# A softmax over 512 columns: the three-row tile moves from the head of the work to its end

## The chip, the cores and the metric

The kernel runs on one core of one Trainium2 chip. The metric is the device time of one execution in microseconds (us); lower is better. Durations in this document come from a hardware profile of one execution; PE is TensorE, DVE VectorE, ACT ScalarE, POOL GpSimd and SP SyncE.

## The reference

The input is one array of 16 x 1024 rows with 512 float32 values each. Every row is halved and put through a softmax:

```python
def reference(x: np.ndarray) -> np.ndarray:
    temp = 2.0
    x_scaled = x / temp
    x_max = np.max(x_scaled, axis=-1, keepdims=True)
    exp_x = np.exp(x_scaled - x_max)
    return (exp_x / np.sum(exp_x, axis=-1, keepdims=True)).astype(np.float32)
```

The input is 33.55 MB and the output as much. Each byte is read once and written once.

## The kernel before

The 16,384 rows are 128 rows on each of the 128 partitions, and "row" below means one such row of 512 values on all partitions, 256 KB. The rows are cut into ten tiles, listed in `TILES` (L10) with their number of rows and their place in `arena`, an on-chip buffer of 98 rows: tiles of 3 and 5 rows, and then eight of 15. Each tile is one contiguous piece of memory. The last two tiles, 8 and 9, go to places that earlier tiles have used; `LATE` (L14) says which stores must have landed before: those of tiles 0, 1 and 2 for tile 8, that of tile 3 for tile 9.

The work of a tile goes over four engines.

- **Loads** (`load`, L113). SP issues the load of tile 0 and ACT that of tile 1 ahead of the opening barrier (`early`, L153). Behind the barrier ACT issues the loads of tiles 2 to 7 (`loads`, L157), one after the other, with no wait. POOL issues those of tiles 8 and 9 (L176 to L179): it first waits until the exponentials of 83 rows are done (`TURN`), and then for the stores in `LATE`. The tile numbered `SPREAD`, tile 1, is loaded in three transfers: all rows but the last over 128 partitions, then the last row over 126 partitions, and over the remaining 2.
- **Exponentials** on ACT, in place, one instruction for each row; it also writes the row's sum to `stats`. The kernel takes exp(x/2) without subtracting the maximum first. Three rows of the first tile are written out (L201 to L208), and the rest runs in a loop over chunks of `E` = 5 rows (`exponentials`, L259). Before each chunk ACT waits for a count that PE raises when a tile has landed (L193, L194).
- **Reciprocal and multiply** on DVE (L166, L169), over up to three chunks of one tile at once, so 15 rows in one multiply; in the last tile each chunk of 5 is multiplied by itself.
- **Stores** on SP, tile by tile in order (`store`, L135), each waiting for its tile's last multiply.

Each engine's order is thus fixed by the program text, and the engines meet at semaphores only. Transfers run on three queues: SP's (q1 in the profile), ACT's (q10) and POOL's (q0). Within a queue they start in the order in which they were issued.

At the end the kernel tests that all sums were in a sound range (L180 to L190). A flag is read by DVE, ACT and POOL when the last store but one has landed (`rounds`, L142 to L148); if a sum had been out of range, a second path with the maximum subtracted would follow. With this input it doesn't run. SP ends by waiting for all stores (L256, L257).

Of the kernel before, what the change touches and what calls it, by code (L numbers as in the profile page):

```python
# [7 lines left out]


TILES = [  # L10
    (3, 0), (5, 3), (15, 8), (15, 23), (15, 38), (15, 53), (15, 68), (15, 83), (15, 0), (15, 15),
]

LATE = {8: (0, 1, 2), 9: (3,)}  # L14
ARENA = 98

HEAD = [3]
E = 5

SPREAD = 1  # L20

TURN = 83

LO, HI = 1.0, 1.0e30
G = 64
# [3 lines left out]
def kernel(  # L29
# [5 lines left out]
    nc = tc.nc  # L35
# [3 lines left out]
    Exp = mybir.ActivationFunctionType.Exp  # L39
# [6 lines left out]
    n_rows = N // P  # L46
    assert sum(r for r, _ in TILES) == n_rows

    arena = nc.alloc_sbuf_tensor("arena", (P, ARENA, D), fp32)
    stats = nc.alloc_sbuf_tensor("stats", (P, n_rows), fp32)  # L50
# [10 lines left out]
    for r, at in TILES:  # L61
        assert at == base % ARENA
        tiles.append((base, r, at))
        base += r

    def dram(ap, t):
        b, r, _ = tiles[t]
        return ap[b * P : (b + r) * P].rearrange("(p r) d -> p r d", r=r)

    def sb(t):  # L70
        _, r, at = tiles[t]
        return arena[:, at : at + r, :]

    straight = sum(HEAD)
    sizes = HEAD + [E] * ((n_rows - straight) // E)
    starts = [sum(sizes[:k]) for k in range(len(sizes))]
    assert sum(sizes) == n_rows
    owner = [max(t for t, (b, _, _) in enumerate(tiles) if b <= s) for s in starts]
# [12 lines left out]
    ld = [nc.alloc_semaphore(f"ld{t}") for t in range(len(tiles))]  # L91
    s_home = {t: nc.alloc_semaphore(f"s_home{t}") for t in LATE}
    s_near = nc.alloc_semaphore("s_near")
    s_end = nc.alloc_semaphore("s_end")
    s_exp = nc.alloc_semaphore("s_exp")
    s_go = nc.alloc_semaphore("s_go")
# [16 lines left out]
    def load(eng, t):  # L113
        r = tiles[t][1]
        parts = [(0, P, 0, r)]
        if t == SPREAD:
            parts = [(0, P, 0, r - 1), (0, 126, r - 1, r), (126, P, r - 1, r)]
        for p, q, lo, hi in parts:
            eng.dma_start(  # L119
                out=sb(t)[p:q, lo:hi], in_=dram(xf, t)[p:q, lo:hi]  # L120
            ).then_inc(ld[t], 16)

    stored_by = {u: s_home[t] for t, us in LATE.items() for u in us}
    for t, (_, r, at) in enumerate(tiles):
        over = {u for u, (_, ru, au) in enumerate(tiles[:t]) if at < au + ru and au < at + r}
        assert over <= {u for v, us in LATE.items() if v <= t for u in us}

# [11 lines left out]
    def take(eng, sem, n):  # L139
        eng.wait_ge(sem, n).then_inc(sem, -n)  # L140
# [11 lines left out]

    def early():  # L153
        load(nc.sync, 0)
        load(nc.scalar, 1)

    def loads():  # L157
        for t in range(2, min(LATE)):
            load(nc.scalar, t)

    def program():

        for j, ks in enumerate(pairs):
            b, c = starts[ks[0]], sum(sizes[k] for k in ks)
            a = b % ARENA
            nc.vector.reciprocal(  # L166
                out=recip[:, b : b + c], in_=stats[:, b : b + c]
            )._wait_ge(s_exp, ks[-1] + 1).then_inc(s_rec, 1)
            nc.vector.tensor_mul(  # L169
                out=arena[:, a : a + c],  # L170
                in0=arena[:, a : a + c],
                in1=recip[:, b : b + c].unsqueeze(2).to_broadcast([P, c, D]),
            )._wait_ge(s_rec, j + 1).then_inc(s_mul, 1)

        nc.gpsimd.memset(ones[:, :], 1.0).then_inc(s_ones, 1)  # L175
        nc.gpsimd.wait_ge(s_exp, starts.index(TURN))  # L176
        for t, us in LATE.items():
            nc.gpsimd.wait_ge(s_home[t], landings(us))
            load(nc.gpsimd, t)  # L179
        nc.gpsimd.tensor_scalar(  # L180
            out=inside[:, :], in0=stats[:, :], scalar1=LO, scalar2=HI,
            op0=Alu.max, op1=Alu.min,
        )._wait_ge(s_exp, len(sizes)).then_inc(s_cnt, 1)
        nc.vector.scalar_tensor_tensor(  # L184
            out=inside[:, :], in0=inside[:, :], scalar=1.0, in1=stats[:, :],
            op0=Alu.mult, op1=Alu.is_equal, accum_out=count[:, :],
        )._wait_ge(s_cnt, 1).then_inc(s_cnt, 1)
        nc.vector.tensor_scalar(  # L188
            out=flag[:, :], in0=total[:, :], scalar1=float(N), scalar2=None, op0=Alu.is_ge,
        )._wait_ge(s_tot, 1).then_inc(s_flag, 1)  # L190


        for t in range(len(tiles)):  # L193
            nc.tensor.wait_ge(ld[t], 48 if t == SPREAD else 16).then_inc(s_go, owner.count(t))  # L194
        nc.tensor.wait_ge(s_ones, 1)
        nc.tensor.matmul(  # L196
            total[:, :], lhsT=count[:, :], rhs=ones[:, :], start=True, stop=True
        )._wait_ge(s_cnt, 2).then_inc(s_tot, 1)

        nc.scalar.preload_act_table(Exp)  # L200
        for k, c in enumerate(HEAD):  # L201
            take(nc.scalar, s_go, 1)
            for b in range(starts[k], starts[k] + c):
                ins = nc.scalar.activation(  # L204
                    out=arena[:, b], in_=arena[:, b], func=Exp, scale=0.5,
                    accum_out=stats[:, b : b + 1],
                )
            ins.then_inc(s_exp, 1)  # L208
        exponentials(straight, n_rows)

        for t in range(len(tiles)):
            store(nc.sync, t)

        x_g = xf.rearrange("(t p r) d -> t p r d", p=P, r=G)
        o_g = of.rearrange("(t p r) d -> t p r d", p=P, r=G)
        data = arena[:, 0:G]

        def vector():  # L220
            for i in range(n_rows // G):
                nc.vector.reduce_max(
                    out=g_max[:, :], in_=data, axis=mybir.AxisListType.X, negate=True
                )._wait_ge(g_go, i + 1).then_inc(g_top, 1)
                nc.vector.reduce_sum(
                    out=g_sum[:, :], in_=data, axis=mybir.AxisListType.X
                )._wait_ge(g_exp, i + 1).then_inc(g_add, 1)
                nc.vector.reciprocal(
                    out=g_sum[:, :], in_=g_sum[:, :]
                )._wait_ge(g_add, i + 1).then_inc(g_rec, 1)  # L230

        def scalar():
            for i in range(n_rows // G):
                nc.scalar.activation(out=data, in_=data, func=Exp, scale=0.5)._wait_ge(
                    g_sub, i + 1
                ).then_inc(g_exp, 1)

        def gpsimd():
            nc.gpsimd.wait_ge(s_end, at_end)
            for i in range(n_rows // G):  # L240
                nc.gpsimd.dma_start(out=data, in_=x_g[i]).then_inc(g_ld, 16)
                nc.gpsimd.wait_ge(g_ld, 16 * (i + 1)).then_inc(g_go, 1)
                nc.gpsimd.tensor_add(
                    out=data, in0=data, in1=g_max[:, :].unsqueeze(2).to_broadcast([P, G, D])
                )._wait_ge(g_top, i + 1).then_inc(g_sub, 1)
                nc.gpsimd.tensor_mul(
                    out=data, in0=data, in1=g_sum[:, :].unsqueeze(2).to_broadcast([P, G, D])
                )._wait_ge(g_rec, i + 1).then_inc(g_mul, 1)
                nc.gpsimd.wait_ge(g_mul, i + 1)
                nc.gpsimd.dma_start(out=o_g[i], in_=data).then_inc(g_st, 16)  # L250
                nc.gpsimd.wait_ge(g_st, 16 * (i + 1))

        rounds(nc.vector, vector)
        rounds(nc.scalar, scalar)
        rounds(nc.gpsimd, gpsimd)
        nc.sync.wait_ge(s_near, 16)  # L256
        nc.sync.wait_ge(s_end, at_end)  # L257

    def exponentials(first, end):  # L259
        row = nc.scalar.alloc_register(f"row{first}")  # L260
        nc.scalar.reg_mov(row, first)
        with nc.scalar.While(lambda: nc.scalar.snap(row, min_val=first, max_val=end) < end):
            now = nc.scalar.snap(row, min_val=first, max_val=end - E)
            take(nc.scalar, s_go, 1)
            at = nc.s_assert_within(
                now % ARENA, 0, ARENA - E,
                skip_runtime_bounds_check_because="no chunk reaches over the arena's end",
            )
            for r in range(E):
                data = arena[:, r : ARENA - E + 1 + r][:, bass.ds(at, 1)]  # L270
                ins = nc.scalar.activation(  # L271
                    out=data, in_=data, func=Exp, scale=0.5,
                    accum_out=stats[:, r : n_rows - E + 1 + r][:, bass.ds(now, 1)],
                )
            ins.then_inc(s_exp, 1)
            nc.scalar.reg_add(row, row, E)
# [45 lines left out]
```

## Time and profile before

| | us |
|---|---|
| median of 3 runs | 167.96 |
| lowest and highest of the 3 | 159.97, 169.0 |
| span of the profiled execution | 158.7 |
| DVE busy | 73.2 |
| ACT busy | 80.8 |
| ACT: one exponential of a row (L271) | 0.615 |
| DVE: one multiply of 15 rows (L169) | 8.16 |
| DVE: one multiply of 5 rows, of 3 rows (L169) | 2.83, 1.76 |
| first store issued; last store issued | 10.94; 143.66 |

The span goes from the first instruction to the last one, and no time beside it is given for the profiled execution; the lowest of the three runs is 1.3 us longer than this span. Busy times of different engines overlap. The time of a transfer isn't in the engines' busy time: it is in the rows for the DMA and in the queue's waits.

### The profile page before, as it was taken

How to read it: one execution, taken by the hardware profiler on the slowest of the kernel's cores; microseconds unless marked ns; L12 is line 12 of the kernel's file. 1: busy time of each engine (PE TensorE's matmuls, PEld its weight loads, DVE VectorE, ACT ScalarE, POOL GpSimd, SP SyncE). 2: the span in 40 equal slices, each digit the busy share in tenths (PEclk: the TensorE clock that was granted, in tenths of full speed). 3: DMA queues.
4: the chain of work that ended last, by engine and by line, in shares of the span. 5: the costliest groups of instructions: out<-in, count | busy, mean ns of one | idle time of the engine just before them, and what ended most of it. 6: DMA issues, size and time to landing. Idle time of an engine off the chain costs nothing. (4 is left out here: it accounts for less than half of the span.)

```text
span 158.7 us, 657 instructions
## 1 busy us (share of the span) xinstructions
PE 0.2 (0%) x2; PEld 0.1 (0%) x2; DVE 73.2 (46%) x27; ACT 80.8 (51%) x257; POOL 2.2 (1%) x8
## 2 busy tenths in 40 slices
PE   0000000000000000000000000000000000000000
PEld 0000000000000000000000000000000000000000
DVE  0047001992981990059500991008932981992000
ACT  0590598697498008940399001991597009940000
POOL 0000000000000000000000300000000000010000
DMA  7999998989999999999999999999999999999995
GB/s 271 382 496 396 463 437 324 480 382 485 410 457 410 457 410 449 418 449 418 441 426 441 426 434 434 426 441 426 441 418 449 418 449 410 457 403 465 403 457 256
DMA packets 3024, 67.11 MB, mean 423 GB/s; under 512 B 336, under 2 KB 336, under 8 KB 720
## 3 DMA queue, kind: packets, MB, share of 16 engines
q1 hardware_dynamic: 1584, 34.34, 50.4%
q10 hardware_dynamic: 1152, 24.90, 37.1%
q0 software_dynamic: 288, 7.86, 11.5%
HBM read 33.55 MB, written 33.55 MB: 423 GB/s over the span
## 5 line engine op out<-in xcount | busy, mean ns | idle before, releaser
L271 ACT ACTIVATE arena<-arena x125 | 76.8, 615 | 54.1 <-ACTq L140 54.1
L169 DVE TENSOR_TENSOR arena<-arena,recip 128x7680 f32<-128x7680 f32 (+2 forms) x12 | 70.2, 5847 | 0.4
L166 DVE RECIPROCAL recip<-stats 128x15 f32<-128x15 f32 (+2 forms) x12 | 2.7, 224 | 70.4 <-ACT arena L271 61.4
L271 ACT ACTIVATION_READ_ACCUMULATOR arena<-arena x125 | 23.4, 187 | 0.0
L200 ACT ACT_TABLE_LOAD x1 | 1.3, 1283 | 5.7 <-issue 5.7
L119 POOL DMA_DIRECT2D arena<-in_x_dram x2 | 1.3, 638 | 84.9 <-ACT arena L271 84.9
L204 ACT ACTIVATE arena<-arena 128x512 f32<-128x512 f32 x3 | 1.9, 619 | 0.0
L180 POOL TENSOR_SCALAR inside<-stats 128x128 f32<-128x128 f32 x1 | 0.6, 630 | 51.7 <-ACT arena L271 51.7
L204 ACT ACTIVATION_READ_ACCUMULATOR arena<-arena 128x1 f32 x3 | 0.6, 188 | 0.0
L196 PE MATMUL total<-ones,count 128*1 128x1 f32 x2 | 0.2, 164 | 143.9 <-DVE inside L184 143.9
L184 DVE SCALAR_TENSOR_TENSOR inside<-inside,stats 128x128 f32<-128x128 f32 x1 | 0.3, 282 | 0.0
L188 DVE TENSOR_SCALAR flag<-total 1x1 int32<-1x1 f32 x1 | 0.1, 146 | 0.3 <-PE total L196 0.3
L196 PEld LDWEIGHTS total<-ones,count 128*1 128x1 f32 x2 | 0.1, 80 | 143.9 <-DVE inside L184 143.9
L175 POOL MEMSET ones<- 128x1 f32 x1 | 0.1, 98 | 2.2 <-POOLq L37 2.2
L306 POOL MEMSET const-bfloat16-1.0<- 128x1 bf16 x1 | 0.1, 108 | 0.0
L306 POOL MEMSET const-uint8-127<- 128x1 uint8 x1 | 0.1, 108 | 0.0
L306 POOL MEMSET const-float32-0.0<- 128x1 f32 x1 | 0.1, 104 | 0.2 <-issue 0.2
L306 POOL MEMSET const-float32-1.0<- 128x1 f32 x1 | 0.1, 104 | 0.0
L184 DVE DVE_READ_ACCUMULATOR inside<-inside,stats 128x1 f32 x1 | 0.1, 80 | 0.0
## 6 DMA issues: line engine op xcount, KB each, us to landing
out_dram<-arena SPq DMA_DIRECT2D x8, 3840.0 KB, 26.2
arena<-in_x_dram ACTq DMA_DIRECT2D x6, 3840.0 KB, 46.7
arena<-in_x_dram POOLq DMA_DIRECT2D x2, 3840.0 KB, 33.6
out_dram<-arena SPq DMA_DIRECT2D x1, 1280.0 KB, 22.9
arena<-in_x_dram ACTq DMA_DIRECT2D x1, 1024.0 KB
arena<-in_x_dram SPq DMA_DIRECT2D x1, 768.0 KB, 5.6
out_dram<-arena SPq DMA_DIRECT2D x1, 768.0 KB, 14.6
arena<-in_x_dram ACTq DMA_DIRECT2D x1, 252.0 KB
```

The source lines that it names most:

```text
L119: eng.dma_start(out=sb(t)[p:q, lo:hi], in_=dram(xf, t)[p:q, lo:hi]).then_inc(ld[t], 16)
L166: nc.vector.reciprocal(out=recip[:, b : b + c], in_=stats[:, b : b + c])._wait_ge(s_exp, ks[-1] + 1).then_inc(s_rec, 1)
L169: nc.vector.tensor_mul(out=arena[:, a : a + c], in0=arena[:, a : a + c], in1=recip[:, b : b + c].unsqueeze(2).to_broadcast([P, c, D]),)._w ...
L175: nc.gpsimd.memset(ones[:, :], 1.0).then_inc(s_ones, 1)
L180: nc.gpsimd.tensor_scalar(out=inside[:, :], in0=stats[:, :], scalar1=LO, scalar2=HI, op0=Alu.max, op1=Alu.min,)._wait_ge(s_exp, len(sizes) ...
L184: nc.vector.scalar_tensor_tensor(out=inside[:, :], in0=inside[:, :], scalar=1.0, in1=stats[:, :], op0=Alu.mult, op1=Alu.is_equal, accum_ou ...
L188: nc.vector.tensor_scalar(out=flag[:, :], in0=total[:, :], scalar1=float(N), scalar2=None, op0=Alu.is_ge,)._wait_ge(s_tot, 1).then_inc(s_f ...
L196: nc.tensor.matmul(total[:, :], lhsT=count[:, :], rhs=ones[:, :], start=True, stop=True)._wait_ge(s_cnt, 2).then_inc(s_tot, 1)
L200: nc.scalar.preload_act_table(Exp)
L204: ins = nc.scalar.activation(out=arena[:, b], in_=arena[:, b], func=Exp, scale=0.5, accum_out=stats[:, b : b + 1],)
L271: ins = nc.scalar.activation(out=data, in_=data, func=Exp, scale=0.5, accum_out=stats[:, r : n_rows - E + 1 + r][:, bass.ds(now, 1)],)
L306: nc = _bacc.Bacc("TRN2", target_bir_lowering=False, num_devices=1)
```

## The change

The tiles are now six of 15 rows, one of 5, two of 15, and the tile of 3 rows last. The buffer has 95 rows instead of 98. SP's load of tile 0 has 15 rows and is the only one ahead of the opening barrier. ACT issues the loads of tiles 1 to 6 behind it. Tile 1 is still the one that is loaded in three transfers, and has 15 rows, so 14 rows go over 128 partitions and one over 126 and 2. POOL issues three loads, those of tiles 7, 8 and 9, each of which waits for one earlier store (0, 1 and 2), and it begins once 80 rows have been through ACT. The loop on ACT takes rows 0 to 124, and the last three rows are written out behind it. DVE cuts only the last tile by chunks as before; that tile has a single chunk of 3 rows now, and the tile of 15 rows before it is multiplied in one instruction.

```diff
 TILES = [
-    (3, 0), (5, 3), (15, 8), (15, 23), (15, 38), (15, 53), (15, 68), (15, 83), (15, 0), (15, 15),
+    (15, 0), (15, 15), (15, 30), (15, 45), (15, 60), (15, 75), (5, 90), (15, 0), (15, 15), (3, 30),
 ]
-LATE = {8: (0, 1, 2), 9: (3,)}
-ARENA = 98
+LATE = {7: (0,), 8: (1,), 9: (2,)}
+ARENA = 95
-HEAD = [3]
+TAIL = 3
-TURN = 83
+TURN = 80
...
-    straight = sum(HEAD)
-    sizes = HEAD + [E] * ((n_rows - straight) // E)
+    turned = n_rows - TAIL
+    sizes = [E] * (turned // E) + [TAIL]
...
     def early():
         load(nc.sync, 0)
-        load(nc.scalar, 1)
     def loads():
-        for t in range(2, min(LATE)):
+        for t in range(1, min(LATE)):
             load(nc.scalar, t)
...
-        for k, c in enumerate(HEAD):
-            take(nc.scalar, s_go, 1)
-            for b in range(starts[k], starts[k] + c):
-                ins = nc.scalar.activation(
-                    out=arena[:, b], in_=arena[:, b], func=Exp, scale=0.5,
-                    accum_out=stats[:, b : b + 1],
-                )
-            ins.then_inc(s_exp, 1)
-        exponentials(straight, n_rows)
+        exponentials(0, turned)
+        take(nc.scalar, s_go, 1)
+        for b in range(turned, n_rows):
+            a = b % ARENA
+            ins = nc.scalar.activation(
+                out=arena[:, a], in_=arena[:, a], func=Exp, scale=0.5,
+                accum_out=stats[:, b : b + 1],
+            )
+        ins.then_inc(s_exp, 1)
```

More of the change, by code (lines that the diff above doesn't have):

```diff
@@ L272, in exponentials @@
                     out=data, in_=data, func=Exp, scale=0.5,
-                    accum_out=stats[:, r : n_rows - E + 1 + r][:, bass.ds(now, 1)],
+                    accum_out=stats[:, r : end - E + 1 + r][:, bass.ds(now, 1)],
                 )
```

## The prediction

> **What bounds the kernel now.** I read the page's slices first, then the byte totals, then the queue's own waits and the timeline at both ends. The first fence is the page: the DMA engines' busy tenths in 40 slices of 3.97 us, what they moved, and the totals.
>
> ```profile
> DMA  7999998989999999999999999999999999999995
> GB/s 271 382 496 396 463 437 324 480 382 485 410 457 410 457 410 449 418 449 418 441 426 441 426 434 434 426 441 426 441 418 449 418 449 410 457 403 465 403 457 256
> ...
> q1 hardware_dynamic: 1584, 34.34, 50.4%
> q10 hardware_dynamic: 1152, 24.90, 37.1%
> q0 software_dynamic: 288, 7.86, 11.5%
> HBM read 33.55 MB, written 33.55 MB: 423 GB/s over the span
> ```
>
> To be seen: the engines that move data are full from the second slice to the last but one. q1 is SyncE's queue (first load, all stores), q10 ScalarE's (loads), q0 GpSimd's (the two late loads). The second fence cuts the span into three stretches; the last two columns are the DMA share and GB/s.
>
> ```profile
> 0.00:7.94 7.94, 0.00 (x0) 0.00 (x0) 0.00 (x0) 2.26 (x4) 0.31 (x5) 1.00 0.88 326
> 7.94:154.70 146.76, 0.19 (x2) 0.09 (x2) 73.21 (x27) 78.50 (x254) 1.90 (x3) 1.00 1.01 433
> 154.70:158.70 4.00, 0.00 (x0) 0.00 (x0) 0.00 (x0) 0.00 (x0) 0.00 (x0) 1.00 0.59 253
> ```
>
> For 147 us the rate is 433 GB/s, whichever queues carry it and whether they load or store; the trace's packet records say the same, 1.138 us for a 30,720-byte packet in nearly all of q1, q10 and q0. ScalarE and VectorE are busy for half of that. So bytes over rate is the bound: 67.11 MB / 433 GB/s = 155.0 us of the 158.7. Only 3.7 us lie outside: 1.0 before the first packet, about 1.0 of thin flow after it in the first 7.94 us (326 x 7.94 = 2.59 MB, which at 433 takes 6.0 us; 7.94 - 6.0 - 1.0 = 0.9), and 1.7 at the end, of which 0.5 lie between the last packet and the notice that it landed.
>
> The third fence is the queue's own waits, then timeline rows that I use below.
>
> ```profile
> SPq L137 <- DVE arena L169: 137.9, 10, 20.1
> SPq L257 <- DMA out_dram<-arena: 14.7, 1, 14.7
> ```
>
> ```profile
> 87.42 0.25 DVE L166 RECIPROCAL recip<-stats 128x15 f32<-128x15 f32 x1 [9.71 <-ACT arena L271]
> 87.70 1.27 POOL L119 DMA_DIRECT2D arena<-in_x_dram  x2 [84.94 <-ACT arena L271]
> 87.71 8.16 DVE L169 TENSOR_TENSOR arena<-arena,recip 128x7680 f32<-128x7680 f32 x1
> 95.89 0.33 SPq L137 DMA_DIRECT2D out_dram<-arena  x1
> ```
>
> SyncE's 137.9 us of waiting for multiplies look like a compute bound and are none, because loads fill the wires meanwhile. At the end the compute chain stops at 144.3 and stores run on for 14.7 us: the store of tile 8 landed at 149.6, that of tile 9, issued at 143.7, at 158.7. One 15-row tile (3.93 MB) alone takes 9.1 us, and two queues that share take 18.2 for each.
>
> **The times.** The span is 158.7. The lowest of the three runs is 159.97, 1.3 above it; the median, 167.96, is 9.3 above it, and no row of the page has these other 8 us. My sum is made against the profiled execution, 158.7 + 1.3 = 160.0, which is 4.7% under the median.
>
> **The change, part by part.**
>
> *Bytes.* The same 128 rows go in and out, and the same 256 KB row goes over 126 and 2 partitions. Nothing is gained or lost in the 155.0 us.
>
> *Start.* SyncE's load, issued at 0.0, is now 3.93 MB instead of 0.77. Its first packet came at 1.0 and will again. ScalarE's loads move behind the opening barrier; there its 15-row loads were issued from 2.66, and without its three early issues (0.13 to 1.49) in front of the barrier I expect about 1.5 to 2. An early ScalarE issue at 0.13 had its first packet at 2.4, so q10 begins near 4. Till then q1 is alone; it holds 9.1 us of work, which hides this. If a lone queue streams at 433, as q1 does from 150 on, the 0.9 us of thin flow go; bounds 0 to -0.9, and above nothing if the lone queue is as poor as tile 0's load was (rivals). I take -0.9, since large packets cause the difference and rows of them all show 1.138.
>
> *First store.* Tile 0 lands when? 3.0 us of its 9.1 go alone by 4.0, the other 6.1 at half rate: 4 + 12.2 + 0.5 = 16.7. ScalarE takes 15 x 0.615 = 9.2 (an ACTIVATE starts each 0.615), VectorE 0.25 + 8.16: store 0 is issued near 34.8. Before, small stores went out from 10.9, and the first 15-row one at 35.5. What replaces these 2 MB of early stores? Loads: ScalarE's queue holds enough for 1.0 + 95 rows x 0.607 = 58.7 us alone. Hidden completely.
>
> *Middle.* From 35.8 q1 and q10 share. Tiles 0, 1, 2 and 7.4/9.1 of tile 3 are in; tile 3 lands at 39, 4 at 57, 5 at 75.5, 6 (5 rows) at 82. GpSimd is let go by 80 rows' exponentials, near 79 (before: 83 rows, 87.7), and needs store 0 (lands 54), store 1 (72), store 2 (near 89). An issue at 87.7 had its first packet at 92.7, so q0 begins near 84: tile 7 lands at 102, tile 8 at 120, and tile 9, three rows, near 124. The third GpSimd issue costs its 0.6 us beside other work; GpSimd's next duty, L179 of the changed kernel, waits for the last exponential anyway.
>
> *End.* Is q1 ever dry? By 124 about 53.1 MB are moved, 33.5 in and 19.6 out: 75 of 128 rows; tile 4's store is ending. From there stores run alone: 5 ends at 134, 6 at 137, 7 at 146, 8 at 155, 9 at 157. Tile 7's multiply ends at 102 + 9.3 + 8.4 = 120, wanted at 137: cover 17. Tile 8, no longer cut into thirds, is multiplied by 138.5, its packets begin at 139.5, wanted at 146: cover 6.5. Tile 9 is done by 141, wanted at 155. Before, the last tile's cover was 149.6 - 144.7 = 4.9. So the last three-row tile removes no wait: a 14.7 us tail of stores was running regardless. What is late next is tile 8's multiply, 6.5 us away. VectorE's reciprocals and multiplies fall from 24 to 20 instructions, worth under 1 us off the path.
>
> *Check of the result.* L148 waits for the last store but one; its load and branch ended 1.24 us later (149.58 to 150.82). The last store used to hide that by 7.9 us, now by 3 rows x 0.607 - 1.24 = 0.6. With that cover gone it costs 1.2 at most. I take 0.
>
> Sum: 158.7 - 0.9 = **157.8 span, 159.1 us** with 1.3 around it. Against 160.0 that is -0.6%, against the median -5.3%. Two per cent is about what a measurement of this kernel can tell from no change.
>
> Two rules of the Trainium skill bear on this. *DMA: Bandwidth & Descriptors*, section "Anatomy of one DMA", gives each transfer some 2.0 us fixed beside its bytes over 436 GB/s; by it the 768 KB store at the end would add 2.0, an estimate from that page, and the sum would be 161.1. The trace speaks against it for queued stores: store 9 landed 9.1 us after store 8, its bytes alone.
>
> *SBUF — State Buffer*, section "Who interferes with whom", says that GpSimd's descriptor writing starves while VectorE runs in two-port modes, but is not stopped by a two-input multiply. The trace agrees: q0's first packet came at 92.7, inside the multiply of 87.71 to 95.87.
>
> **Rivals.**
>
> *The last 8 us of the median stay* (0.33). Whatever lay around or inside the two longer runs is not touched: 157.8 + 9.3 = 167.1, no measurable change. For it: two of three runs, and a change that leaves bytes and rate alone. Against: the profile shows 158.7 as what the program needs. I put 0.42 on 159.1 and 0.33 here; no row decides between them, only that the sum can be made for one and not for the other.
>
> *Small or lone transfers do not stream* (0.05). Tile 0's 768 KB took 4.6 us from first packet to landing, 170 GB/s, sharing with q10 from 2.4. At that rate the 3 us of a lone q1 would lose 3 x (1 - 170/433) = 1.8, giving 161.8 instead of the gain; the last store at 4.6 instead of 1.8 adds 2.8: 162 to 164.6 in all.
>
> *A dry tail, slower* (0.16). GpSimd's loads of tiles 7 and 8 are held behind VectorE. Price: each of two issues held for one multiply, 8.16 us, puts tile 8 16.3 us later; its cover is 6.5, so 9.8 us are lost: 168.9 by the profiled execution, 176.9 with the median's surroundings. It decides from a slip of 6.5 us on, one for one, and is over 2% slower than the median at 10.7 with those surroundings. For it: 33 rows now go by q0, and the last long tile is unsplit. Against: 92.7 inside a multiply, and a slip of loads lets stores run earlier.
>
> The remaining 0.04 is shared by the signs. **Chances**: faster 0.47 (0.42 + 0.05), same 0.35 (0.33 + 0.02), slower 0.18 (0.16 + 0.02). The likeliest case's own range is 157.7 (1.3 around 156.4, if half the end loss goes too) to 161.8. With the case of 167.1, whose longest run here lay 1.0 above the median, the range is 157.5 to 169.0 and leaves out most of the slower cases, under 2 in 10.
>
> **What would show it.** Right: the first slice over 300 GB/s and the second over 400; first store issued at 33 to 37; GpSimd's issues from 76 to 92; no slice under 380 between; the last multiply near 141; SyncE's last wait 14 to 18 us. Wrong: a slice under 300 near 140 to 146 (dry tail), a last slice nearly empty (check not hidden), or 30,720-byte packets slower than 1.138 us throughout, which no step here foresees.

## The result and the profile after

The changed kernel takes **162.72 us** (162.33 to 163.1), the kernel before 159.97: 1.0175 times as long, with a 95% interval of 1.0165 to 1.0185. It is slower by 2.75 us, under the 2% that I had called measurable and clear of the noise all the same. Two of the three times shown of before were some 8 us longer than this kernel's usual time, and every comparison here leaves out such runs, which are over 1.5% above the fastest of their kernel, so the 167.96 of the table is not what the change is measured against.

The span of the profiled execution grew from 158.7 to 161.4. The page of the changed kernel, in the lines that answer to the first fence of the prediction:

```profile
DMA  8999999989999999999999999999999999999993
GB/s 297 415 449 403 421 413 404 472 381 480 388 464 419 442 404 449 426 426 429 447 388 431 358 426 449 426 434 442 411 442 414 442 454 388 452 442 434 434 391 146
...
q1 hardware_dynamic: 1584, 37.49, 54.7%
q10 hardware_dynamic: 1008, 20.97, 30.6%
q0 software_dynamic: 432, 8.65, 12.8%
HBM read 33.55 MB, written 33.55 MB: 416 GB/s over the span
```

The transfers are as busy as before; no slice is empty, and yet the mean fell from 423 to 416 GB/s. Two slices stand out: the 23rd (89 to 93 us) with 358, and the last with 146. The windows of the changed kernel (last columns again DMA share and GB/s) put sizes to this; the first three rows are the start, the fourth the stretch around the weak slice, the last two the end. The fence behind them is the kernel before in the stretch of the fourth row:

```profile
0.00:7.94 7.94, 0.00 (x0) 0.00 (x0) 0.00 (x0) 1.28 (x1) 0.31 (x5) 1.00 0.93 358
7.94:18.00 10.06, 0.00 (x0) 0.00 (x0) 0.00 (x0) 0.00 (x0) 0.00 (x0) 1.00 0.98 425
18.00:24.00 6.00, 0.00 (x0) 0.00 (x0) 0.00 (x0) 5.21 (x17) 0.00 (x0) 1.00 1.02 396
...
84.00:93.50 9.50, 0.00 (x0) 0.00 (x0) 7.62 (x2) 3.51 (x11) 0.00 (x0) 1.00 0.97 378
155.00:157.00 2.00, 0.00 (x0) 0.00 (x0) 0.00 (x0) 0.00 (x0) 0.00 (x0) 1.00 0.84 359
157.00:162.00 5.00, 0.00 (x0) 0.00 (x0) 0.00 (x0) 0.00 (x0) 0.00 (x0) 1.00 0.34 143
```

```profile
84.00:93.50 9.50, 0.00 (x0) 0.00 (x0) 6.04 (x2) 3.39 (x12) 1.27 (x2) 1.00 1.00 430
```

These windows count a packet's bytes where the packet starts, so a short window is off by up to the packets in flight at its ends. Where it matters, a packet's bytes are spread over its time below, and the time lost is reckoned against 433 GB/s.

- **Start.** The first 7.94 us show 358 GB/s instead of 326, which would be worth (358 - 326) x 7.94 / 433 = 0.6 us. Spread over their time, the packets leave 0.1 of it: by 7.94 us the kernel before has lost 2.1 us and the changed one 2.0, because the first 16 packets of the lone load took 1.36 to 2.45 us. At 18 to 24 us another 0.5 us goes. The packet records show 16 loads in flight there, each taking some 1.5 us instead of 1.138, right behind the 2,048-byte packets of the row over 126 and 2 partitions. The kernel before had the same spell (a short stretch of slow packets) behind the same packets at 6.5 us. It was moved, not removed. The kernel before then loses 0.4 us at 24 to 28 us, and by 28 us both have lost 2.6: next to nothing was gained.
- **84 to 93.5 us.** By the window, (433 - 378) x 9.5 / 433 = 1.2 us are lost; spread over their time, the packets lose 1.0 from 80 to 95, and the kernel before nothing. SyncE's store packets take up to 1.95 us there, and then GpSimd's load packets up to 2.08, instead of 1.138. The first store packets over 1.3 us come at 77, beside the five-row tile's packets and ahead of GpSimd's first at 84.62.
- **End.** The 5 us behind 157 are a third full, because some of the 16 transfer engines are done long before others. A transfer counts as landed when its last part has. The 16 parts of the last store, from the trace's landing records, in us:

```
before  157.73 157.82 157.87 157.91 157.93 157.94 157.97 157.98 158.03 158.10 158.11 158.13 158.15 158.25 158.30 158.66
after   158.35 158.50 158.51 158.58 158.59 158.61 158.80 158.83 159.00 159.26 159.37 159.42 159.44 160.80 161.30 161.36
```

The mean landing went from 158.06 to 159.30, by 1.24, and the lag of the last part behind the mean from 0.6 to 2.1, by 1.45. Together they are the 2.7 us. Both arise mainly in one place: the parts of tile 5's load still land within 1.9 us of each other (74.3 to 76.2), those of the five-row tile's within 5.0 (86.5 to 91.5) and those of tile 7's, loaded behind 84 us, within 4.1 (102.8 to 106.9). The last store's are still 3.0 apart.

The queue's waits and the timeline of GpSimd and VectorE in the changed kernel:

```profile
SPq L137 <- DVE arena L168: 140.6, 10, 35.2
SPq L256 <- DMA out_dram<-arena: 15.9, 1, 15.9
```

```profile
80.01 1.27 POOL L119 DMA_DIRECT2D arena<-in_x_dram  x2 [78.47 <-ACT arena L270]
93.55 0.53 POOL L119 DMA_DIRECT2D arena<-in_x_dram  x1 [12.27 <-DMA out_dram<-arena]
138.29 5.42 POOL L179 TENSOR_SCALAR inside<-stats 128x128 f32<-128x128 f32 x1 [44.20 <-ACT arena L204]
```

```profile
135.05 8.16 DVE L168 TENSOR_TENSOR arena<-arena,recip 128x7680 f32<-128x7680 f32 x1
143.33 1.76 DVE L168 TENSOR_TENSOR arena<-arena,recip 128x1536 f32<-128x1536 f32 x1
```

The first store was issued at 36.58, GpSimd's first loads at 80.01, tile 8's multiply ended at 143.21, while the store of tile 7 ran until 150.4: the tail was never dry (the store queue never ran out of work near the end), and compute set nothing.

### The profile page after: what moved, and what is told of

Read it like the earlier page. It is cut to its first block, busy times and chain, and to the rows that moved or that the text cites. A ratio compares the mean times of both kernels' runs of the same rounds, so it can differ in the third digit from the quotient of the medians.

```text
span 161.4 us, 653 instructions
## 1 busy us (share of the span) xinstructions
PE 0.2 (0%) x2; PEld 0.1 (0%) x2; DVE 72.5 (45%) x23; ACT 80.4 (50%) x257; POOL 7.5 (5%) x9
## 5 line engine op out<-in xcount | busy, mean ns | idle before, releaser
L179 POOL TENSOR_SCALAR inside<-stats 128x128 f32<-128x128 f32 x1 | 5.4, 5417 | 44.2 <-ACT arena L204 44.2
L119 POOL DMA_DIRECT2D arena<-in_x_dram x3 | 1.8, 602 | 90.7 <-ACT arena L270 78.5
L195 PE MATMUL total<-ones,count 128*1 128x1 f32 x2 | 0.2, 164 | 145.4 <-DVE inside L183 145.4
```

The lines of the kernel that those rows point to most:

```text
L119: eng.dma_start(out=sb(t)[p:q, lo:hi], in_=dram(xf, t)[p:q, lo:hi]).then_inc(ld[t], 16)
L179: nc.gpsimd.tensor_scalar(out=inside[:, :], in0=stats[:, :], scalar1=LO, scalar2=HI, op0=Alu.max, op1=Alu.min,)._wait_ge(s_exp, len(sizes) ...
L195: nc.tensor.matmul(total[:, :], lhsT=count[:, :], rhs=ones[:, :], start=True, stop=True)._wait_ge(s_cnt, 2).then_inc(s_tot, 1)
```

## The experiments

At 84 to 93.5 us three things meet: the five-row tile, whose packets of 10,240 bytes start on ScalarE's queue from 75 to 88; GpSimd's first packets, from 84.6; and stores. Theory A blamed small packets meeting GpSimd's, theory B GpSimd's larger share of loads, theory C the late first store or the short last one.

### GpSimd's loads later

```diff
-TURN = 80
+TURN = 95
```

> The changed kernel with TURN = 95 instead of 80, so GpSimd's first late load waits until the exponentials of all first 95 rows are done; that keeps the five-row tile's 10,240-byte packets on ScalarE's queue and GpSimd's packets apart in time. Theory A (the loss arises where these small packets meet GpSimd's first packets and SyncE's stores, at 84 to 93 us of the changed kernel): about 160.0, 2.7 under the changed kernel's 162.7, and no slice under 400 GB/s between 80 and 100 us; the cover of tile 8's multiply, 5.7 us, shrinks by the 8 to 12 us of later loads, so up to 4 us may come back as a dry tail. Theory B (GpSimd's three loads of 33 rows are the cost, whenever they run): 162.7 or more. Theory C (the later first store, or the short last store, is the cost): 162.7.

Measured: 167.36 us, 1.0503 times before. The slices of this kernel's page:

```profile
GB/s 296 404 451 446 409 363 474 407 422 459 392 452 444 385 459 452 385 452 432 407 439 452 444 370 452 407 444 422 422 437 437 412 402 468 437 200 0 355 474 308
```

and two rows of its timeline on VectorE:

```profile
145.10 0.25 DVE L165 RECIPROCAL recip<-stats 128x15 f32<-128x15 f32 x1 [8.97 <-ACT arena L270]
145.39 8.16 DVE L168 TENSOR_TENSOR arena<-arena,recip 128x7680 f32<-128x7680 f32 x1
```

The weak spell at 84 to 93 is gone (a smaller one, 370, stands at 96 to 100), and a hole of about 6.7 us, by the packet records, has opened at 148 to 154.5 (200, then 0): GpSimd issues at 92.7, tile 8's multiply begins at 145.4 and ends at 153.5, and its store has nothing ahead of it in the queue. This is the dry tail that the prediction described, 6.7 us of it where the expectation allowed 4. The rest, 166.0 - 6.7 = 159.3, would be 2.1 under the changed kernel, but that doesn't speak for A: in the hole the engines that were ahead waited for the others, and the parts of the last store land within 0.2 us of each other (165.78 to 165.96). By the mean landing, 165.9 - 6.7 = 159.2 stands against 159.3 in the changed kernel. This run decides nothing between the theories.

### The five-row tile third

```diff
-    (15, 0), (15, 15), (15, 30), (15, 45), (15, 60), (15, 75), (5, 90), (15, 0), (15, 15), (3, 30),
+    (15, 0), (15, 15), (5, 30), (15, 35), (15, 50), (15, 65), (15, 80), (15, 0), (15, 15), (3, 30),
```

> The changed kernel with the five-row tile as the third tile instead of the seventh, everything else as it was (same loads by GpSimd, same TURN). Theory A: GpSimd's packets now meet 30,720-byte packets on ScalarE's queue, as in the kernel before, so about 160.0 and landings of the 16 parts of each late tile within 1.5 us of each other (4.1 in the changed kernel). Theory B: 162.7, since GpSimd's loads are the same. Theory C: 162.7.

Measured: 160.18 us, 1.002 (1.0009 to 1.003). The loss of 2.75 is down to 0.3 by moving one short tile. This kernel's windows:

```profile
75.00:84.00 9.00, 0.00 (x0) 0.00 (x0) 7.43 (x1) 2.32 (x7) 0.54 (x1) 1.00 0.97 418
84.00:93.50 9.50, 0.00 (x0) 0.00 (x0) 2.47 (x2) 7.81 (x27) 0.53 (x1) 1.00 1.00 428
155.00:157.00 2.00, 0.00 (x0) 0.00 (x0) 0.00 (x0) 0.00 (x0) 0.00 (x0) 1.00 0.70 292
157.00:162.00 5.00, 0.00 (x0) 0.00 (x0) 0.00 (x0) 0.00 (x0) 0.00 (x0) 1.00 0.13 53
```

428 GB/s where the changed kernel had 378, and a short end; the last store's parts land from 157.78 to 158.75. GpSimd's three loads, the late first store and the three-row last store are all still there: B and C are out.

### The same short tile in the kernel before

```diff
-    (3, 0), (5, 3), (15, 8), (15, 23), (15, 38), (15, 53), (15, 68), (15, 83), (15, 0), (15, 15),
+    (3, 0), (15, 3), (15, 18), (15, 33), (15, 48), (15, 63), (15, 78), (5, 93), (15, 0), (15, 15),
-LATE = {8: (0, 1, 2), 9: (3,)}
+LATE = {8: (0, 1), 9: (2,)}
```

> The kernel before with its five-row tile moved from the second to the eighth place, just ahead of GpSimd's two late loads; its first load stays three rows, its last tile 15. Theory A: it loses what the changed kernel lost, 162 to 163 against 160.0. Theories B and C: 160.0, within 0.5, since late loads, first store and last store stay those of the kernel before.

Measured: 161.59 us, 1.012 (1.0102 to 1.0138), with runs from 160.0 to 162.1. The direction is A's, the size a good half of it. Its profiled execution was the shortest of these runs and shows no slow packets beside the five-row tile's load (86.6 to 97.7 us), so where its other runs lose is not seen.

### Without the row over 126 and 2 partitions

```diff
-SPREAD = 1
+SPREAD = -1
```

> The changed kernel with tile 1 loaded in one transfer of 15 rows over 128 partitions, with no row over 126 and 2. In the changed kernel all 16 loads in flight slowed to about 320 GB/s for 1.5 us right behind those 2,048-byte packets, at 20 to 22 us. If the small packets cause that, it goes and the time falls by 0.5 to 162.2; if the row relieves two engines that are late at the end, the time rises by up to 0.7 to 163.4. Theories A, B and C say nothing else of it: the 84 to 93 us loss stays.

Measured: 161.44 us, 1.3 under the changed kernel. The spell at 20 us went, and one of 0.7 us came up at 40 to 45. The gain came from elsewhere: by the packet records, the stretch from 80 to 95 us cost 0.15 us on average instead of 1.0. No transfer in that stretch had been changed. They came about 1 us earlier (GpSimd's first packet at 83.78 instead of 84.62), and the 16 engines may have stood differently to each other when they got there; which of these counted isn't shown.

### Small packets without a short tile, first attempt

On the kernel with the five-row tile third:

```diff
+        if t == 6:
+            parts = [(0, P, 0, 5), (0, P, 5, 10), (0, P, 10, r)]
```

PE's wait for this tile is raised to the 48 landings of three transfers.

> The kernel with the five-row tile third (160.2), and now its tile 6, the 15 rows that ScalarE's queue loads while GpSimd's packets begin, in three transfers of 5 rows each, so its packets have 10,240 bytes instead of 30,720. Tiles, order, TURN and bytes stay. Theory A, small packets on ScalarE's queue beside GpSimd's packets: the loss comes back, 162 to 164, with late tiles' 16 landings 3 us or more apart. Theory A2, the place of the short tile matters by its timing and not by its packets: 160.2 within 0.5.

Measured: 160.68 us: 0.5 over 160.18, a quarter of the least that A wanted, and no packet of 30,720 bytes took over 1.2 us beside the small ones, which ran from 63.5 to 103. Two kernels further down lose as much with no small loads beside stores, so this answer is inconclusive; the question is taken up again at the end.

### GpSimd's loads earlier

```diff
-TURN = 80
+TURN = 70
```

> The changed kernel with TURN = 70 instead of 80: GpSimd issues its first load some 7 us earlier, so its packets lie beside nearly all of the five-row tile's 10,240-byte packets and not beside the second half alone. Theory A, with a loss that grows with the overlap: 163.5 to 165. Theory A2, a chance meeting at one point of time: anything from 160 to 162.7.

Measured: 160.92 us. GpSimd's packets now begin at 70.5 us and the small ones run from 78.8 to 98.3, and the loss against the kernel before shrank to 1.0. A, with GpSimd's packets as the partner, has fallen.

### Eight tiles of 16 rows

```diff
+    (16, 0), (16, 16), (16, 32), (16, 48), (16, 64), (16, 80), (16, 0), (16, 16),
+LATE = {6: (0,), 7: (1,)}
+ARENA = 96
+TAIL = 0
+E = 4
```

With these values the code of the three-row tail goes, and a tile's four chunks of 4 rows share one multiply, but for the last tile's.

> The changed kernel's order with eight tiles of 16 rows in a buffer of 96 rows: chunks of 4 rows, no three-row tile, no five-row tile, two late loads by GpSimd of 16 rows each; the last tile is multiplied in chunks of 4. No small packets but those of the row over 126 and 2. Theory A: 159.5 to 160.2, as GpSimd's packets meet 32,768-byte packets alone. A dry tail would show as slices under 350 near 145 us and add its length.

Measured: 160.59 us, 0.4 over what was expected at most. No short tile, and most of the loss is gone. It does not beat the kernel before.

### Five rows third, without the row over 126 and 2

> The kernel with the five-row tile third (160.2), tile 1 in one transfer. If the row over 126 and 2 costs 0.5 us at 20 us wherever the five-row tile stands, and nothing takes its place: 159.7. In the changed kernel leaving it out gained 1.3, but the loss of 0.5 at 20 us came back as 0.7 at 40 to 45 us, so most of that gain lay at 84 to 93 us; if that is general, there is nothing left to gain here: 160.2 to 160.5.

The edit is the one line `SPREAD = -1` on that kernel. Measured: 160.69 us. The spell at 20 us went again, and spells of 1.0 us together came up at 36 to 44. Without that row nothing is gained here.

### Three tests of a lottery

Theory P: any shift of the engines against each other counts, so times scatter. Theory Q: three queues at work while the short tile is the last on its queue.

```diff
-TURN = 80
+TURN = 85
```

> The changed kernel with TURN = 85: GpSimd starts about 3 us later than with 80, its first packets near 88, when the five-row tile on ScalarE's queue is ending. Theory P (the 16 transfer engines hold a pattern of start times among themselves; each event that shifts it costs a spell of slow packets until they have a workable pattern again, and how much depends on the pattern they carry, so the 84 to 93 us loss is a matter of that pattern and of when GpSimd's first packets arrive): a time other than 162.7, between 160 and 163, with the slow packets again at GpSimd's first packets. Theory Q (three queues at work while the short tile is the last on ScalarE's queue always costs 2.5): 162.7 within 0.4.

Measured: 162.74 us (161.58 to 163.42), the changed kernel's time, as Q wanted; four of the 16 parts of the last store land at 161.3 to 161.8, the others by 159.0.

```diff
-SPREAD = 1
+SPREAD = 3
```

> The changed kernel with the row over 126 and 2 partitions in tile 3's load instead of tile 1's: the same packets, some 28 us later, so the pattern in which the engines arrive at 84 us differs and nothing else does at that place. Theory P: the loss at 84 to 93 changes; leaving the row out altogether brought it from 1.0 to 0.15 us on average and the lag of the last engines from 2.1 to 1.5, so 160 to 162.2. Theory Q: 162.7 within 0.4.

Measured: 162.2 us, at the edge of both theories. The slow packets are back at 88 to 92 us, the lag of the last engines is smaller (1.2 us in the profiled execution, the shortest of the four).

> The kernel before with TURN = 73 instead of 83: GpSimd's loads start 6 us earlier, beside a 15-row tile on ScalarE's queue as before, and both late loads come earlier. Theory P: no need for a short tile, any time from 159.9 to 162. Theory Q: 159.9 within 0.3, since no short tile is near.

The edit is `TURN = 73` in the kernel before. Measured: 159.99 us, ratio 1.0008 (0.9997 to 1.002). With no short tile among the mixed transfers, an earlier release of GpSimd costs nothing. How far its start moved in these runs isn't seen: the execution that was profiled is not among those compared, and in it GpSimd issued at 86.12 (87.70 before) and its first packet came at 92.69, as before.

### Five rows sixth

```diff
+    (15, 0), (15, 15), (15, 30), (15, 45), (15, 60), (5, 75), (15, 80), (15, 0), (15, 15), (3, 30),
```

> The changed kernel with the five-row tile sixth instead of seventh, so the last load on ScalarE's queue is one of 15 rows; GpSimd is released by the same 80 rows, now the end of the five-row tile. Theory P: 160 to 161.5, as with five rows third (160.2). Theory Q: 160.2 within 0.4, and the same by a theory that only wants the short tile not to be last on its queue.

Measured: 163.15 us, 1.0203 (1.0176 to 1.023). The short tile is not the last on its queue and lands before GpSimd's first packets, and the loss is at least as large: Q has fallen, and with it any need for three queues. Slow packets stand at 64 to 73 us, around the short tile's end. Most of this loss is lag: in the profiled execution the mean landing of the last store is 158.81, 0.75 later than in the kernel before, and its last part is 3.1 behind that mean.

### Fourth and fifth place, and another start of GpSimd

Theory R: a short tile costs when it is loaded beside stores, and not while loads run alone. The first two edits move the five-row tile in the list as before; the third is `TURN = 70` on the kernel with five rows third.

> The changed kernel with the five-row tile fourth: its load ends near 33 us, while loads still run alone (the first store is issued at 36.6). Theory R (a short tile costs when it is loaded beside stores, and not while loads run alone; third, it is loaded alone and costs nothing, sixth and seventh beside stores and costs 2.5 to 3): 160.2 within 0.4. Theory P (any shift of the engines' pattern counts, so places are a lottery): anything from 160 to 163.

> The changed kernel with the five-row tile fifth: loaded from about 39 us on, beside the first store, and some 35 us ahead of GpSimd's first packets. Theory R: 162 to 163.2, with the slow packets at 40 to 60 us and none at 84. Theory P: anything from 160 to 163. If three queues at work were needed, 160.2.

> The kernel with the five-row tile third and TURN = 70 instead of 80. In the changed kernel that TURN took 1.8 away, with the short tile beside stores. Theory R: the moment at which GpSimd starts matters only with a short tile in flight, so 160.2 within 0.3. Theory P: a shift of GpSimd's start moves the time either way, 160 to 162.

Measured: fourth 160.23 us (159.98 to 160.56), fifth 161.8 (160.2 to 163.12), third with the other start 160.23 (160.04 to 160.33). Third and fourth, loaded by 33 us, before the first store is issued: no loss, also with GpSimd's first packet 5 us earlier (73.63 instead of 78.40). In the fifth place three of the seven runs lie at 160.2 to 160.4 and lose nothing, and four at 161.8 to 163.1; the comparison counts six of them, without the 163.12, and their median is 161.1. So fifth, sixth and seventh, beside stores, are 0.9, 3.0 and 2.5 over 160.2. R holds for the fourth place and for the third, and in part for the fifth, which misses R's 162 by 0.9: how much is lost, and whether anything is, varies from run to run of one kernel. P's free lottery is narrowed: the kernels that shift things without small loads beside stores stay within 0.5 of each other.

### Small packets without a short tile, again

On the kernel with five rows third, as above, with tile 5 or tile 4 in three transfers instead of tile 6 (`if t == 5`, `if t == 4`, and PE's wait to match).

> The kernel with the five-row tile third (160.2), and tile 5, a 15-row tile loaded beside stores at about 62 to 80 us, in three transfers of 5 rows each: 10,240-byte packets at the place where the five-row tile itself cost most (sixth, 163.2), with no tile shorter than 15 rows there. If 10,240-byte packets beside stores are what costs: 161.5 to 163.5. If it takes a short tile, whose end shifts the loads against the stores by a third of a tile: 160.7, as with tile 6 in three transfers.

> The same with tile 4, loaded beside the first stores at about 44 to 62 us, in three transfers of 5 rows (the five-row tile itself cost 1.6 in this stretch, as the fifth tile). If 10,240-byte packets beside stores are what costs: 161 to 163. If it takes a short tile: 160.7 or less.

Measured: tile 5 161.12 us, tile 4 162.87. The slices of the kernel with tile 5 in three transfers, and below them those with tile 4:

```profile
GB/s 284 419 439 408 399 421 418 446 415 446 415 448 438 423 443 395 413 446 466 423 446 415 454 400 469 392 484 384 477 384 477 394 427 435 424 484 261 492 369 320
```

```profile
GB/s 259 445 457 389 402 443 396 457 380 477 375 469 444 403 464 388 479 373 474 383 441 479 373 479 358 464 388 479 373 487 414 452 425 388 464 441 411 472 358 119
```

The small packets ran elsewhere than expected: tile 5's from 45 to 75 us and tile 4's from 33 to 49. In the first kernel the slice of 261 is a dry tail. While small loads and stores run together, the engines take one packet of each in turn: from 48 to 64 us the packet records have some 170 of 10,240 bytes beside 168 of 30,720, so the loads get a quarter of the bytes. Tile 5 landed at 76.9 instead of 64.3, all later loads came later with it, tile 8's multiply ended at 147.4, and for 1.2 us hardly a packet was in flight. That accounts for its 0.9 us, and no packets were stretched beside the small loads. So this run doesn't show what it was sent for. In the second the loss is back in full, in a kernel whose tiles and order alone take 160.18: small load packets can do it with no short tile at their place. Two of the three pieces of its tile 4 had landed by 39.9, before the first store's first packet at 40.06, and only the third ran beside stores, where the five-row tile runs when it is fifth. But no slice there is very weak. By the packet records the small loads at 40 to 48 us lose next to nothing while they run; some 0.3 us go by 60, and 0.5 more at 96 to 101, where all packets have 30,720 bytes. One part of the last store lands at 161.44, the other 15 by 159.85.

In one table, over the 160.2 of the three kernels in its first row, whose small loads run alone:

| small load packets beside stores | us | over 160.2 |
|---|---|---|
| none: five rows third, fourth, third with TURN 70 | 160.18, 160.23, 160.23 | 0.0 |
| none: five rows third without the row over 126 and 2; eight tiles of 16 rows | 160.69, 160.59 | 0.5, 0.4 |
| tile 6, tile 5, tile 4 in three transfers | 160.68, 161.12 (1.2 a dry tail), 162.87 | 0.5, 0.9, 2.7 |
| five rows fifth, sixth, seventh | 161.1 (six runs, 160.2 to 162.2), 163.15, 162.72 | 0.9, 3.0, 2.5 |
| seventh with TURN 70, with TURN 85 | 160.92, 162.74 | 0.7, 2.5 |
| seventh, row over 126 and 2 left out, in tile 3 | 161.44, 162.2 | 1.2, 2.0 |

**What is shown**: the five-row tile's place among the loads makes the difference of the two kernels. Loaded while loads run alone it costs nothing, and loaded beside stores it cost 0.7 to 3.0 us, by the medians, in the changed kernel and all six variants of it whose tail was not dry (in the fifth place not in every run); in the kernel before the same move cost 1.6. None of the kernels without small loads beside stores lost over 0.5 against 160.2, by the medians too.

**What stays open**: what is wrong with it there. Small packets of a 15-row tile cost 2.7 at one place, and at two others nothing that stands out from the 0.4 and 0.5 lost without them. How much a kernel loses, and when, depends on things as far off as a row loaded 60 us earlier, which points to how the 16 engines stand to each other; that is argued from these scatterings, not shown. What stretches a 30,720-byte packet from 1.138 to 2 us in such spells, and why it sets single engines 2 to 3 us back, no run here tells. That they stay back fits engines that are never out of work: only the two kernels with a dry tail end with the parts of the last store within 0.2 us of each other. The small *stores* of the five-row tile, on SyncE's queue beside loads at 75 to 92 us of the kernel with five rows third, cost nothing (428 GB/s above).

## The prediction, point by point

- **The bound**: half right. Bytes over rate sets most of the time in all kernels, and the 155 us stay. What it left out: the end is the slowest of 16 engines, each with a sixteenth of the bytes, and the profile's rate is their mean. In the kernel before that difference was 0.6 us and looked like part of the fixed end.
- **Start, -0.9**: this term came to nothing. I took the thin flow for a matter of small packets, but the lone load's first 16 packets, of 30,720 bytes, were slow too (1.36 to 2.45 us), and the spell behind the 2,048-byte packets, which I had counted as thin flow at the start, only moved to 20 us. By 28 us both kernels had lost 2.6 us. The 0.9 itself was read from a window; with the packets spread over their time, the kernel before lost 1.1 between its first packet and 7.94 us.
- **First store**: issued at 36.6, inside 33 to 37, at no cost, as said. The three kernels of the table's first row have it as late and end within 0.3 of the kernel before.
- **Middle**: this is the step that failed. "tile 6 (5 rows) at 82" moved a tile of 10,240-byte packets from a stretch where it met little into one where loads and stores share the engines, and I gave it no price. It measured 2.5 us (seventh against third place). In the two profiles the mean landing of the last store is 1.2 later, 1.0 of it from stretched packets at 80 to 95 us, and the lag of the last part behind that mean 1.4 longer. Its time was wrong too: two queues were to share evenly, but from 77 to 84 us ScalarE's queue moved 0.79 MB beside 2.18 MB of SyncE's, 77 packets beside 71, and the tile's parts landed from 86.5 to 91.5. I took the 433 over 147 us as proof that any mixture streams at the full rate; a mean over so long a stretch hides a spell such as the one at 24 to 28 us of the kernel before (324 GB/s in the 7th slice, 0.4 us by the packet records). That spell was no clear hint at small packets: its first slow loads start at 24.67, ahead of the first 10,240-byte packet of the five-row store at 25.89.
- **End**: right in that stores were never short of work, but the cover was smaller than 6.5. Tile 8's last part landed at 125.1 (120 expected) and its multiply ended at 143.2 (138.5 expected). With TURN = 95 that multiply ended at 153.5, 10.3 later, and left a hole of 6.7, which puts the cover at some 3.6 us, an estimate from these two runs.
- **The check**: hidden, right. Its branch ended at 160.3, the last landing came at 161.4.
- **The rivals**: the dry tail gave the right sign for a wrong reason. The small or lone transfers gave a sum that holds the measured time, 162 to 164.6, by luck: the lone load lost 0.9 us by 4 us, half of the 1.8 it was priced at and no more than the start before, and the small last store did stream. The first part of that store landed 1.8 us behind the first part of the store before it (156.51 to 158.35), which is its bytes at 433 GB/s. The 2 us fixed for each transfer by the Trainium skill, *DMA: Bandwidth & Descriptors*, section "Anatomy of one DMA", which measured them on GpSimd's path while this store is on SyncE's, are not in these traces at the end: the kernel with five rows third has the same 768 KB store last, and its landing comes 1.9 us behind that of the store before it (156.86 to 158.75). The last 8 us of the median did not stay: the six runs of the changed kernel lie between 162.33 and 163.1.
- **The range**: half of the 1.7 us at the end, taken off 157.8, gives 156.95 and not 156.4, so the likeliest case's lower end would have been 158.25 instead of 157.7. Nothing hangs on it.
- **What would show it**: "no slice under 380 between" was named among the signs that the sum is right, and 358 came. Near misses were the first slice (297, not over 300), GpSimd's last issue (93.55, not by 92) and the last multiply (over at 145.1, not near 141). Packets of 30,720 bytes slower than 1.138 us "throughout" were named as a sign that it is wrong; they came mainly in one spell.

## What to carry to other kernels

When transfers are the bound, look at the landings of a transfer's 16 parts as well as at GB/s: the end belongs to the slowest engine, and a stretch of a few us can put single engines behind to the end. Here a short tile cost nothing when it was loaded while loads ran alone, and 0.7 to 3 us beside stores, so in such a kernel one that must exist is best loaded before the first store. A start that is made cleaner may only move its cost: the spell at 6.5 us came back at 20, and without the row over 126 and 2 spells came at 36 to 45.

## What was not expected

GpSimd's L179 took 5.42 us in the changed kernel, against 0.63 for the same instruction (L180) before, because it fell into VectorE's 8.16 us multiply of tile 8 (135.05 to 143.21), and ended 0.5 us behind it. L180 had begun at 140.65, just ahead of a multiply:

```profile
140.58 0.19 DVE L166 RECIPROCAL recip<-stats 128x5 f32<-128x5 f32 x1
140.81 2.83 DVE L169 TENSOR_TENSOR arena<-arena,recip 128x2560 f32<-128x2560 f32 x1
```

```profile
140.65 0.63 POOL L180 TENSOR_SCALAR inside<-stats 128x128 f32<-128x128 f32 x1 [51.67 <-ACT arena L271]
```

That agrees with the Trainium skill, *SBUF — State Buffer*, section "Who interferes with whom", by which a two-input VectorE operation contends with GpSimd's reads. It cost nothing: it was over at 143.7, and the result's check waits until the last store but one has landed at 159.5.

GpSimd's loads had their first packet 4.6 to 5.0 us after issue (80.01 to 84.62; 87.70 to 92.68), against 1.0 for SyncE's first load.
